# Retention: state updates of four batches as 32-row products on four row tiles

## The chip, the cores and the metric

The kernel runs on one core of a Trainium2 chip. The metric is the device time of one execution in microseconds (us), as the median of several runs. The engines appear as PE (TensorE), DVE (VectorE), ACT (ScalarE), POOL (GpSimd) and SP (SyncE, which here only issues DMAs).

## The reference

One inference step of a decoder trunk of two layers, for one prompt of 256 tokens and eight samples of 4 tokens each (256 + 32 = 288 token columns). Layer 0 mixes by causal pooling, layer 1 by retention; each layer then has a convolutional FFN and a gated embedding. What the change touches is the retention of the samples, for each of 8 heads with key width 256 and value width 512:

```python
sc = jnp.einsum('bhnk,bhmk->bhnm', qc, kc) * intra
o = (jnp.einsum('bhnm,bhmv->bhnv', sc, vc)
     + jnp.einsum('bhnk,bhkv->bhnv', qc, S) * cross[None, :, :, None])
S = sdec[None, :, None, None] * S + jnp.einsum('bhmk,bhmv->bhkv', kc * kdec[None, :, :, None], vc)
```

For the samples, `S` is a given state of 256 x 512 for each of the 8 batches and 8 heads, and the new one is an output: 64 states of 512 KB are read, used and written. `o` is then normalised over its 512 values, multiplied by `silu(g)` and projected.

## The kernel before

All matrix work keeps weights stationary and moves the 288 token columns. Every float32 operand is split into a high and a low part of type fp32r, and `three` (line 270) issues three products: high x high, high weight x low, low weight x high. A weight piece of 256 x 512 is loaded (`dma`, line 1429, on SP, five buffers), split by ScalarE (`split_hi`, line 1435) and VectorE (`split_lo`, line 1443), two pieces ahead of its use. The main loop goes through the pieces in order; for each of 4 output blocks `m` it issues six products and then calls `tick`. A `Group` is a set of pieces with the same output; it holds four PSUM banks, from a pool of five (`pbank`), and is emptied by `evac` at its last piece.

Everything else is side work: short operations in two queues, `main` and `side`, which `tick` drains into the instruction streams between main products. The planner keeps an estimated clock per engine. An operation is written down if its PSUM need `nb` is met and it is `timely`: a TensorE operation when its inputs are due by TensorE's clock, another one when its inputs and its engine's clock are at most 500 ns ahead. One drain stops after 900 ns of TensorE work:

```python
while q and q[0].eng != "W" and fits(q) and timely(q[0]) and pe < 900:
    if q[0].eng == "P":
        pe += q[0].cost
    run(q)
```

The order thus written is what each engine executes; real waits are semaphores. Side work draws banks from a second pool of three (`sbank`, first in, first out); `release` puts a bank back at the moment when the last reader is written down, and the hardware waits for that reader.

In retention, a head has a group for q and k (`gA`), one for v (`gB`), four short ones of 4 row blocks for the output projection of head h-2 (`gO`), and one for the gate (`gC`). `attention` (from line 1041) queues the side work of a head. The sample keys and values are stacked four times into 128 rows (a high or low part of all 32 tokens in each 32 rows: `kst`, `vsk`), transposed on TensorE and kept as `ksr` and `vst`. Then, for each batch `b` and each half `kk` of the key width: `sh_` and `sl_` split the state half, `upd` (line 1258) multiplies `Km`, which is `ksr` masked to the rows of batch b (`km_`, line 1254), with `vst`, all 128 rows; `outer` (lines 1274, 1275) adds q x state into one bank `os`, held through all 16 halves; `snew` (line 1262) forms the new state from the old one and the update bank and frees the bank; a store goes out on POOL (line 1265) and the load of a later state on SP (line 1051), three state buffers in all. At the end `osum0` and `osum1` (lines 1324, 1327) bring the output to the tile `on[2]` of 32 rows, `gstat` and `gnorm` normalise, and `otrans` transposes four column blocks, each with two transposes of 128 rows and one of 32 (through line 268). `norm_ops` (lines 321, 322) spreads the row norms with a product of ones; its last part has 32 rows.

Of the kernel before, what the change touches and what calls it, by code (L numbers as in the profile page):

```python
# [32 lines left out]
RAW_BUFS = 5  # L33
SPLIT_BUFS = 3
# [11 lines left out]
def _constants():  # L46
# [39 lines left out]
    c["dm"] = np.where(n >= m, np.exp(lg[:, None, None] * np.maximum(n - m, 0)) / 16, 0).astype(f)  # L86
# [4 lines left out]
    c["gx"] = np.exp(lg[:, None] * (t + 1)[None, :]).astype(f)  # L91
    c["ks"] = (np.exp(lg[:, None] * (3 - t)[None, :]) / 16).astype(f)
# [3 lines left out]
    c["ds"] = np.tile(ds, (4, 1, 1)).astype(f)  # L96
    c["bm"] = np.tile((b[:, None] == np.arange(8)[None, :]).astype(f), (4, 1))
# [14 lines left out]
def trunk_kernel(ctx: ExitStack, tc: tile.TileContext, I: dict, O: dict):  # L112
# [5 lines left out]
    mmp = ctx.enter_context(tc.tile_pool(name="mmp", bufs=5, space=bass.MemoryType.PSUM))  # L118
    msp = ctx.enter_context(tc.tile_pool(name="msp", bufs=1, space=bass.MemoryType.PSUM))

    def pbank():
        return mmp.tile([128, 512], F32, tag="mm", name="mm")

    banks = [msp.tile([128, 512], F32, name=f"ms{i}") for i in range(3)]
    free = deque(banks)

# [23 lines left out]
    side = deque()  # L150
    ready = set()
# [3 lines left out]
    class Op:  # L155
        __slots__ = ("eng", "cost", "fn", "nb", "key", "dep", "end")

        def __init__(self, eng, cost, fn, nb=0, key=None, dep=()):
            self.eng, self.cost, self.fn, self.nb, self.key, self.dep, self.end = eng, cost, fn, nb, key, dep, 0.0

# [34 lines left out]
    def fits(q):  # L195
        op = q[0]
        return op.nb <= len(free) and (op.key is None or op.key in ready)

    def inputs(op):
        return max((d.end for d in op.dep), default=0.0) + LAT  # L200
# [27 lines left out]
    def tick():  # L228
        drain(main)
        drain(side)  # L230

    def step():
        if main and fits(main):
            run(main)
        elif side and fits(side):
            run(side)
        else:
            raise RuntimeError("nothing can run")

    def force(cond):  # L240
        while not cond():
            step()

# [54 lines left out]
    def norm_ops(ph, dep=()):  # L298
# [68 lines left out]
    class PoolPhase:  # L367
# [47 lines left out]
        def start(self):  # L415
# [11 lines left out]
            px = pbank()  # L427
# [15 lines left out]
            for _ in range(16):  # L443
# [10 lines left out]
                   px.rearrange("p (j c t) -> p c j t", j=4, c=4))  # L454
            w = self.weigh(1) + self.sbg(1)
# [17 lines left out]
        def xT(self, i, q, on_v):  # L473
            ps = pbank()
# [103 lines left out]
    class FfnPhase:  # L578
# [3 lines left out]
        def start(self):  # L582
            force(lambda: not side and "rows" in ready)
# [188 lines left out]
    class PlePhase:  # L772
# [3 lines left out]
        def start(self):  # L776
            force(lambda: not side and ("u", self.l, 21) in ready)
# [31 lines left out]
        def build(self):  # L809
# [26 lines left out]
            def finish():  # L836

                flush()
                sums = [pbank() for _ in range(3)]
# [14 lines left out]
                for m in range(4):  # L854
                    ps = sbank() if m < 3 else pbank()
# [79 lines left out]
    class RetPhase:  # L935
# [5 lines left out]
        def start(self):  # L941
            force(lambda: not side and "x15" in ready)
# [7 lines left out]
            self.gx, self.ks = t("gx", [128, HEADS, 32]), t("ks", [128, HEADS, 32])  # L950
            self.ds, self.bm = t("ds", [128, HEADS, 32]), t("bm", [128, 8])
            GP.dma_start(self.kd, I["kd"])
            GP.dma_start(self.gx, I["gx"].partition_broadcast(128))
            GP.dma_start(self.ks, I["ks"].partition_broadcast(128))
            GP.dma_start(self.ds, I["ds"])
# [3 lines left out]
            GP.memset(self.qb.bitcast(F32), 0.0)  # L959
            self.mv = t("mv", [128, 3, 2])  # L960
# [7 lines left out]
            self.kst = t("kst", [128, 2, 4, 32])  # L968
            self.krp = t("krp", [128, 2, 4, 32])
# [4 lines left out]
            self.vsk = t("vsk", [128, 4, 4, 32])  # L974
            self.vst = t("vst", [128, DV], F32R)
            self.ssf = t("ssf", [128, 32])
            self.ssh = t("ssh", [128, 32], F32R)
            self.sss = t("sss", [128, 32], F32R)
            self.bn = t("bn", [128, 3, 6])
# [63 lines left out]
        def attention(self, h):  # L1043
# [5 lines left out]
            def load_s(b):  # L1049
                s = self.tl("S", [128, 2, DV], 3)  # L1050
                SP.dma_start(s, I["state_ret"][0, b, h].rearrange("(k p) v -> p k v", p=128))
                st["S", b] = s
                ld = Op("D", 0, None)
                at = max(clk["P"], stored[b - 3].end + 2500 if b >= 3 else 0.0)
                ld.end = charge("D", PIECE, at) + 2000
                loaded[b].dep = loaded[b].dep + (ld,)


            def loads():
                st["dm"] = self.tl("dm", [128, 256], 1)  # L1060
                SP.dma_start(st["dm"], I["dm"][h])
                load_s(0)
                load_s(1)
            bc = lambda t: t[:, h].unsqueeze(1).broadcast_to([128, 2, 32])
# [6 lines left out]
            kr = lambda: st["kr"].bitcast(F32)  # L1071
# [8 lines left out]
            loaded, stored = {}, {}  # L1080
            ops.append(Op("N", 0, loads))
            add("krp", oa(256, lambda: A.copy(self.krp, ks.unsqueeze(2).broadcast_to([128, 2, 4, 32]))), "rot")
# [429 lines left out]
```

## Time and profile before

| | |
|---|---|
| median of 3 runs | 3006.28 us (3005.09 to 3008.97) |
| profiled execution | 3006.09 us, span 3004.2 us |
| PE busy | 2985.6 us (99%) |
| PE weight loads busy | 2934.2 us (98%) |
| DVE busy | 1957.9 us (65%) |
| ACT busy | 1415.4 us (47%) |
| POOL busy | 80.7 us (3%) |
| DMA | 542.08 MB, mean 180 GB/s |

The span runs from the first to the last instruction of the profiled execution; its own time also holds what lies around it. Busy shares are means over the whole span. A product's row on PE shows its whole passage through the array; products are pipelined, so the next one starts long before the row ends, and the distance between starts tells what a product costs.

### The profile page before, as it was taken

To read this page: it belongs to the slowest core of one execution; us is meant where nothing else is said; L and a number is where in the kernel's file an instruction comes from. 1 tells how busy PE (TensorE), PEld (TensorE's weight loads), DVE (VectorE), ACT (ScalarE), POOL (GpSimd) and SP (SyncE) were. 2 spreads that over 40 slices of the span, in tenths; PEclk is the share of its full clock that TensorE was granted. 3 is DMA by queue.
4 is the path that set the end of the run, shared out by engine and by line. 5 is a ranking of instruction groups with operands and counts; after the bars stand their busy time and mean duration, and the time that the engine had idled before them with its cause. 6 is when DMAs were issued, how large, how long until landed. Compare 5 with 4: busy or idle time off the path is not lost.

```text
span 3004.2 us, 54263 instructions
## 1 busy us (share of the span) xinstructions
PE 2985.6 (99%) x22007; PEld 2934.2 (98%) x22007; DVE 1957.9 (65%) x3401; ACT 1415.4 (47%) x2142; POOL 80.7 (3%) x129
## 2 busy tenths in 40 slices
PE   8999999999999999999999999999999999999998
PEld 8999999999999999999999999999999999999998
DVE  7666656565666666776766767686666575756565
ACT  6544444444444545444444444455444343434454
POOL 1000000000000000000000000000000000000000
PEclk9999999999999999999999999999999999999999
DMA  7555555555555566665756757565555555555553
GB/s 231 158 164 166 168 162 167 163 166 164 167 175 165 168 217 198 233 232 164 249 192 207 231 170 247 191 192 172 163 167 168 164 165 166 165 166 165 175 159 116
DMA packets 288817, 542.08 MB, mean 180 GB/s; under 512 B 18836, under 2 KB 55652, under 8 KB 288454
## 3 DMA queue, kind: packets, MB, share of 16 engines
q1 hardware_dynamic: 275878, 496.21, 53.6%
q0 software_dynamic: 12688, 42.40, 4.2%
q8 instruction: 173, 2.83, 0.4%
q14 instruction: 78, 0.64, 0.1%
HBM read 496.41 MB, written 42.84 MB: 179 GB/s over the span
## 4 chain that ended last, share of the span: by engine, by line
PE 98%; DMA 1%; DVE 0%; ACT 0%; issue 0%; SPq 0%; ACTq 0%; DVEq 0%
PE mm L271 31%; PE mm L273 30%; PE mm L272 30%; PE ms L268 1%; PE ms L1274 1%; PE ms L1258 1%; PE ms L1275 1%; PE ms L272 0%; PE ms L271 0%; PE ms L273 0%; DMA raw<-in_ret_w_in 0%; PE ms L1090 0%; DMA x<-in_x_prompt 0%; DVE lo L1443 0%; PE mm L268 0%
## 5 line engine op out<-in xcount | busy, mean ns | idle before, releaser
L1435 ACT CAST hi<-raw 128x1024 fp32r<-128x1024 f32 x864 | 907.5, 1050 | 1391.0 <-PE mm L272 1190.8
L271 PE MATMUL mm<-xh,hi 128*128 128x288 f32 x4928 | 1464.4, 297 | 0.0
L272 PE MATMUL mm<-xl,hi 128*128 128x288 f32 x4928 | 1453.9, 295 | 0.0
L273 PE MATMUL mm<-xh,lo 128*128 128x288 f32 x4928 | 1449.1, 294 | 0.0
L1443 DVE TENSOR_TENSOR lo<-raw,hi 128x1024 fp32r<-128x1024 f32 x864 | 1055.7, 1222 | 552.2 <-ACT hi L1435 550.2
L271 PEld LDWEIGHTS mm<-xh,hi 128*128 128x128 f32 x4928 | 923.8, 187 | 11.8
L272 PEld LDWEIGHTS mm<-xl,hi 128*128 128x128 f32 x4928 | 925.3, 188 | 4.7
L273 PEld LDWEIGHTS mm<-xh,lo 128*128 128x128 f32 x4928 | 927.9, 188 | 0.0
L272 PE MATMUL mm<-hl,hi 128*128 128x288 f32 x1408 | 415.4, 295 | 0.0
L273 PE MATMUL mm<-hh,lo 128*128 128x288 f32 x1408 | 415.1, 295 | 0.0
L271 PE MATMUL mm<-hh,hi 128*128 128x288 f32 x1408 | 413.3, 294 | 0.0
L271 PEld LDWEIGHTS mm<-hh,hi 128*128 128x128 f32 x1408 | 264.7, 188 | 0.0
L272 PEld LDWEIGHTS mm<-hl,hi 128*128 128x128 f32 x1408 | 264.7, 188 | 0.0
L273 PEld LDWEIGHTS mm<-hh,lo 128*128 128x128 f32 x1408 | 264.5, 188 | 0.0
L665 DVE SCALAR_TENSOR_TENSOR c<-U,cv,c 128x304 f32<-128x304 f32 x352 | 180.2, 532 | 3.5 <-ACT c L662 0.4
L271 PE MATMUL mm<-rhh,hi 128*128 128x288 f32 x512 | 152.2, 297 | 0.0
L273 PE MATMUL mm<-rhh,lo 128*128 128x288 f32 x512 | 151.5, 296 | 0.0
L272 PE MATMUL mm<-rhl,hi 128*128 128x288 f32 x512 | 149.8, 293 | 0.4 <-DVE rhl L1352 0.4
L755 DVE TENSOR_TENSOR x<-x,mm 128x288 f32<-128x288 f32 x192 | 82.7, 452 | 86.2 <-PE mm L273 86.2
L637 DVE TENSOR_TENSOR U<-mm,rb 128x256 f32<-128x256 f32 x176 | 74.2, 422 | 94.7 <-PE mm L273 94.7
L662 ACT ACTIVATE c<-U,cv 128x304 f32<-128x304 f32 x176 | 107.7, 635 | 15.7 <-DVE U L638 15.7
L1262 DVE SCALAR_TENSOR_TENSOR S<-S,ms 128x512 f32<-128x512 f32 x128 | 87.4, 683 | 36.1 <-PE ms L1258 35.8
(265 smaller groups left out, 2110.8 us busy)
## 6 DMA issues: line engine op xcount, KB each, us to landing
raw<-in_ffn_w_up SPq DMA_DIRECT2D x352, 512.0 KB
raw<-in_ffn_w_down SPq DMA_DIRECT2D x176, 512.0 KB
raw<-in_ret_w_in SPq DMA_DIRECT2D x128, 512.0 KB
raw<-in_ple_w_gate SPq DMA_DIRECT2D x64, 512.0 KB
raw<-in_ret_w_in SPq DMA_DIRECT2D x128, 256.0 KB
S<-in_state_ret SPq DMA_DIRECT2D x64, 512.0 KB
out_ret_s<-S POOLq DMA_DIRECT2D x64, 512.0 KB, 4.4
raw<-in_ret_w_out SPq DMA_DIRECT2D x64, 512.0 KB
```

The lines of the kernel that those rows point to most:

```text
L268: T.transpose(out, in_, ident[:rows, :rows])
L271: T.matmul(out, w[0], a[0], start=start, stop=False)
L272: T.matmul(out, w[0], a[1], start=False, stop=False)
L273: T.matmul(out, w[1], a[0], start=False, stop=stop)
L637: V.tensor_tensor(U[:, s, 2:258], ps[:, 0:256], rb[:, 0:256], MUL)
L662: A.activation(c[0][:, 0:304], u[:, 2:306], AF.Identity, bias=w(3), scale=w(2))
L665: V.scalar_tensor_tensor(c[0][:, 0:304], u[:, s:304 + s], w(s), c[0][:, 0:304], MUL, ADD)
L755: V.tensor_tensor(x[:, M], x[:, M], ps[:, :NT], ADD)
L1258: T.matmul(ps, st["km", b][:, 128 * kk:128 * kk + 128], self.vst, start=True, stop=True)
L1262: V.scalar_tensor_tensor(s[:, kk], s[:, kk], g ** 4, st["u", b, kk], MUL, ADD)
L1435: A.copy(h, raw[i])
L1443: V.tensor_tensor(l, r, h.bitcast(F32), SUB)
```

## The change

- The two PSUM pools become one of eight banks. Main groups take theirs from it too; `kept` reserves those that the current group has yet to take.
- The stacks are ordered by row tile: the 32 rows of tile r hold the high and low parts of batches 2r and 2r+1. `Km` is `ksr` masked to the even or the odd batch of each tile, two masks in place of eight. `upd(par, kk)` issues four products of 32 rows, one for each tile, each into a bank of its own.
- The state halves are tiles of their own, eight buffers, loaded through a third queue, `back`; they go in the order of the update groups. The output is summed in four groups of four halves, each in a bank that `osum` adds to a resident tile `on2` of 128 rows; `fold` adds its rows 32 to 63 to rows 0 to 31. State updates of a group follow among the outputs of the next.
- `otrans` transposes all 128 rows of `on2`; the last part of the spread in `norm_ops` has 128 rows.
- The tables `dm`, `gx`, `ks`, `ds` of a head come in one load `hd`; `kst`, `krp` and `vsk` share a tile; in the last head the fourth update group goes behind the transposes; phases start with `finish_side` in place of a forced drain.

```diff
+    banks = [psp.tile([128, 512], F32, name=f"ps{i}") for i in range(8)]
     free = deque(banks)
+    kept = [0]
...
-        return op.nb <= len(free) and (op.key is None or op.key in ready)
+        return op.nb <= len(free) - kept[0] and (op.key is None or op.key in ready)
...
         drain(main)
         drain(side)
+        drain(back)
...
-            V.tensor_scalar(diag[:32, 256:288], ident[:32, :32], rtok[:32, 2:3], None, MUL)
+            V.tensor_scalar(diag[:, 256:288], ident[:, 0:32], rtok[:, 2:3], None, MUL)
...
-            T.matmul(ps[:, 256:288], ones[:32, :], diag[:32, 256:288], start=True, stop=True)
+            T.matmul(ps[:, 256:288], ones, diag[:, 256:288], start=True, stop=True)
...
+            self.hd = self.tl("hd", [128, 352], 1)
+            SP.dma_start(self.hd, I["hd"][h])
...
+            def load_s(n, dep=()):
+
+                b, kk = where(n)
+                ld = Op("D", PIECE / 2, None, dep=dep, late=3500.0 if dep else 0.0)
...
+            def upd(par, kk):
+                for r in range(4):
+                    rows = slice(32 * r, 32 * r + 32)
+                    ps = st["u", 2 * r + par, kk] = sbank()
+                    T.matmul(ps, st["km", par][rows, 128 * kk:128 * kk + 128], self.vst[rows], start=True, stop=True)
+
+            def snew(n):
+                b, kk = where(n)
+                V.scalar_tensor_tensor(st["S", n], st["S", n], g ** 4, st["u", b, kk], MUL, ADD)
                 release(st["u", b, kk])
...
+                GP.dma_start(O["ret_s"][0, b, h, 128 * kk:128 * kk + 128], st["S", n])
+
+                if n + S_BUFS < 16:
+                    load_s(n + S_BUFS, (o[f"sn{n}"],))
...
+            def outer(n):
+                b, kk = where(n)
+                if n % 4 == 0:
                     st["os"] = sbank()
                 o = st["os"]
                 lq = self.qb[:, kk, 64 * b:64 * b + 64]
...
+                T.matmul(o[:64], lq, st["sh", n], start=n % 4 == 0, stop=False)
+                T.matmul(o[:64], lq, st["sl", n], start=False, stop=n % 4 == 3)
...
+            def osum(u):
+                if u == 0:
+                    A.copy(self.on2[:64], st["os"][:64])
+                else:
+                    V.tensor_tensor(self.on2[:64], self.on2[:64], st["os"][:64], ADD)
+                release(st["os"])
...
+            def new_state(n):
+                add(f"sn{n}", ov(512, lambda: snew(n)), f"up{n // 4}")
+
+            def update(u):
+                add(f"up{u}", op_(430, lambda: upd(u // 2, u % 2), nb=4), "km1 vsk")
+
+            for u in range(4):
+                for n in range(4 * u, 4 * u + 4):
+                    if u > 0:
+                        new_state(n - 4)
+                    add(f"out{n}", op_(460 + (230 if n == 0 else 0), lambda n=n: outer(n), nb=0 if n % 4 else 1),
+                        f"sl{n}" + (" sss vsk" if n == 0 else ""))
+                    if n < 14:
+                        half(n + 2)
+                        half_lo(n + 2)
+                add(f"os{u}", (oa if u == 0 else ov)(512, lambda u=u: osum(u)), f"out{4 * u + 3}")
+                if u < 3 or h < 7:
+                    update(u)
+            add("fold", ov(512, fold), "os3")
...
-                to_tr(ps[:, 256:288], on[2][:32, c], 32)
+                to_tr(ps[:, 256:384], on[2][:, c], 128)
...
             for m in range(4):
                 if j == 0:
-                    g.ps[m] = pbank()
+                    g.ps[m] = sbank()
+                    kept[0] -= 1
...
                     g.evac(m, ps)
+                    release(ps)
```

## Rows read from the trace of the kernel before

**Rows 1.** The page, parts 1 and 4: busy time, chain that ended last.
```profile
PE 2985.6 (99%) x22007; PEld 2934.2 (98%) x22007; DVE 1957.9 (65%) x3401; ACT 1415.4 (47%) x2142; POOL 80.7 (3%) x129
...
PE 98%; DMA 1%; DVE 0%; ACT 0%; issue 0%; SPq 0%; ACTq 0%; DVEq 0%
```

**Rows 2.** One head's stretch: length, PE, PEld, DVE, ACT, POOL busy; clock; DMA.
```profile
1510.00:1634.00 124.00, 124.00 (x880) 118.23 (x879) 85.17 (x148) 58.46 (x89) 6.40 (x9) 1.00 0.65 209
```

**Rows 3.** Waits of PE: who waited for whom, total us, times, longest.
```profile
PE mm L268 <- DMA ident<-in_ident: 5.3, 1, 5.3
...
PE ms L504 <- DVE xl L521: 0.7, 1, 0.7
...
PE mm L272 <- DVE rhl L1352: 0.4, 1, 0.4
```

**Rows 4.** PE by line and form: count, busy us, mean ns, idle before.
```profile
L1258 PE MATMUL ms<-vst,Km 128*128 128x512 f32 x128 | 50.4, 394 | 0.0
...
L268 PE MATMUL ms<-ident,fm 128*128 128x128 f32 x64 | 8.3, 272 | 0.0
...
L268 PE MATMUL ms<-ident,on 32*128 32x32 f32 x32 | 7.8, 244 | 0.0
...
L321 PE MATMUL ms<-acc,ones 128*128 128x256 f32 x10 | 3.1, 388 | 0.5 <-DVE acc L316 0.5
```

**Rows 5.** Timeline of PE in the state work of head 0: start, length, instruction.
```profile
1137.09 0.40 PE L1258 MATMUL ms<-vst,Km 128*128 128x512 f32 x1
...
1138.48 0.29 PE L271 MATMUL mm<-xh,hi 128*128 128x288 f32 x1
1138.61 0.29 PE L272 MATMUL mm<-xl,hi 128*128 128x288 f32 x1
```

**Rows 6.** Timeline of PE at one `otrans`; x3 are merged: two 128-row, one 32-row.
```profile
1151.27 0.55 PE L268 MATMUL ms<-ident,on 128*128 128x128 f32 x3
...
1151.76 0.40 PE L271 MATMUL mm<-xh,hi 128*128 128x288 f32 x1
...
1151.99 0.29 PE L272 MATMUL mm<-xl,hi 128*128 128x288 f32 x1
```

**Rows 7.** Timeline of PE: eight transposes of 128 rows, merged.
```profile
1079.49 1.03 PE L268 MATMUL ms<-ident,fm 128*128 128x128 f32 x8
```

**Rows 8.** Timeline of PE at one spread in `norm_ops`; two 32-row products between.
```profile
79.97 0.59 PE L321 MATMUL ms<-acc,ones 128*128 128x256 f32 x2
...
81.06 0.30 PE L272 MATMUL mm<-xl,hi 128*128 128x288 f32 x1
```

**Rows 9.** Timeline, all engines: an update product and its state update.
```profile
1096.16 0.39 PE L1258 MATMUL ms<-vst,Km 128*128 128x512 f32 x1
...
1096.59 0.69 DVE L1262 SCALAR_TENSOR_TENSOR S<-S,ms 128x512 f32<-128x512 f32 x1
```

**Rows 10.** The same with a weight split of DVE between them.
```profile
1104.62 0.40 PE L1258 MATMUL ms<-vst,Km 128*128 128x512 f32 x1
...
1105.90 0.68 DVE L1262 SCALAR_TENSOR_TENSOR S<-S,ms 128x512 f32<-128x512 f32 x1
```

**Rows 11.** Line L1262 (`snew`): what DVE sat idle for before it, us, times.
```profile
  PE ms L1258: 35.8, 33
```

**Rows 12.** Timeline in the pooling layer: PE waits for a bank that DVE empties.
```profile
23.46 0.18 DVE L521 TENSOR_TENSOR xl<-ms,xh 128x32 fp32r<-128x32 f32 x1
...
23.70 0.30 PEld L504 LDWEIGHTS ms<-pq,x 128*128 128x128 f32 x2 [0.86 <-DVE xl L521]
```

**Rows 13.** DVE by line and form: count, busy us, mean ns, idle before.
```profile
L1254 DVE TENSOR_SCALAR Km<-ksr,bm 128x256 fp32r<-128x256 f32 x64 | 22.9, 358 | 0.0
...
L1015 DVE TENSOR_TENSOR qk<-fm,t 128x576 f32<-128x576 f32 x8 | 6.0, 752 | 0.0
...
L1327 DVE TENSOR_TENSOR on<-on,ms 32x512 f32<-32x512 f32 x8 | 5.4, 669 | 0.0
```

**Rows 14.** Waits of SP's DMA queue: state loads behind state stores.
```profile
SPq L1051 <- DMA out_ret_s<-S: 149.1, 40, 7.4
```

More of the change, by code (lines that the diff above doesn't have):

```diff
@@ L117, in trunk_kernel @@
     wp = ctx.enter_context(tc.tile_pool(name="wp", bufs=1))
[L118 to L124, printed above, removed]
+    psp = ctx.enter_context(tc.tile_pool(name="psp", bufs=1, space=bass.MemoryType.PSUM))
+    banks = [psp.tile([128, 512], F32, name=f"ps{i}") for i in range(8)]
     free = deque(banks)
+    kept = [0]
     def sbank():
@@ L150, in trunk_kernel @@
     side = deque()
+    back = deque()
     ready = set()
@@ L196, in fits @@
         op = q[0]
-        return op.nb <= len(free) and (op.key is None or op.key in ready)
+        return op.nb <= len(free) - kept[0] and (op.key is None or op.key in ready)
     def inputs(op):
-        return max((d.end for d in op.dep), default=0.0) + LAT
+        return max((d.end for d in op.dep), default=0.0) + LAT + op.late
     def run(q):
@@ L236, in step @@
             run(side)
+        elif back:
+            run(back)
         else:
@@ L242, in force, with finish_side @@
             step()
+    def finish_side():
+        while side:
+            if side[0].eng == "W":
+                side.popleft()
+            elif fits(side):
+                run(side)
+            else:
+                step()
     def force_key(k):
@@ L582, in start @@
         def start(self):
-            force(lambda: not side and "rows" in ready)
+            finish_side()
+            force_key("rows")
             l = self.l
@@ L776, in start @@
         def start(self):
-            force(lambda: not side and ("u", self.l, 21) in ready)
+            finish_side()
+            force_key(("u", self.l, 21))
             l = self.l
@@ L838, in finish @@
                 flush()
-                sums = [pbank() for _ in range(3)]
+                sums = [sbank() for _ in range(3)]
                 toks = (slice(0, 128), slice(128, 256), slice(256, 288))
@@ L941, in start @@
         def start(self):
-            force(lambda: not side and "x15" in ready)
+            finish_side()
+            force_key("x15")
             p = self.p = new_pool("ret")
@@ L977, in start @@
             self.ssh = t("ssh", [128, 32], F32R)
+            self.ssg = t("ssg", [128, 32])
             self.sss = t("sss", [128, 32], F32R)
+            self.on2 = t("on2", [128, DV])
+            V.memset(self.on2, 0.0)
             self.bn = t("bn", [128, 3, 6])
@@ L1047, in attention, with where, load @@
             st = {}
[L1049 to L1056, printed above, removed]
-            def loads():
[L1060 to L1064, printed above, removed]
+            dm, gx, sk, ds = (self.hd[:, a:b] for a, b in ((0, 256), (256, 288), (288, 320), (320, 352)))
+            bc = lambda t: t.unsqueeze(1).broadcast_to([128, 2, 32])
+            def where(n):
+                return 2 * (n % 4) + n // 8, (n // 4) % 2
+            def load_s(n, dep=()):
+                b, kk = where(n)
+                ld = Op("D", PIECE / 2, None, dep=dep, late=3500.0 if dep else 0.0)
+                def load():
+                    st["S", n] = self.tl("S", [128, DV], S_BUFS)
+                    SP.dma_start(st["S", n], I["state_ret"][0, b, h, 128 * kk:128 * kk + 128])
+                    here = Op("D", 0, None)
+                    here.end = ld.end + 2000
+                    o[f"sh{n}"].dep += (here,)
+                    ready.add(("S", h, n))
+                ld.fn = load
+                back.append(ld)
+            def loads():
+                for n in range(S_BUFS):
+                    load_s(n, self.stored[n:n + 1])
             qv = [self.qb[:, kk].rearrange("p (b c) -> p b c", c=68) for kk in range(2)]
@@ L1368, in attention @@
             ops += hid
+            if h == 7:
+                update(3)
+                for n in range(12, 16):
+                    new_state(n)
             side.extend(ops)
```

175 lines of the change are left out of this document (82 added, 93 removed).

## Prediction

> **What bounds the kernel now.** The page comes first: TensorE is busy 99% of the span and the chain that ended last is 98% TensorE [rows 1]. Then the table by stretches: in the retention layer one head takes 124 us, TensorE is busy in all of it, VectorE 85 us of it, at the full granted clock [rows 2]. Then TensorE's own waits: the longest are 5.3 us at the start and 0.7 us in the pooling layer, and the only one in retention is 0.4 us [rows 3]. So TensorE is never late: every nanosecond taken from its stream shortens the run, and every nanosecond for which it must wait lengthens it. Work on VectorE, ScalarE and the queues is free until TensorE waits for it. I therefore sum TensorE's stream and new waits. The sum is made against the profiled execution, 3006.09 us (span 3004.2 us plus 1.9 us around it), which stands 0.2 us below the median of the three runs, 3006.28.
>
> **Updates as row tiles.** There are 128 update products [rows 4]. In the timeline two updates and four output products run from 1137.09 to 1138.48, 1.39 / 6 = 0.232 us a product [rows 5]: 128 x 0.232 = 29.7 us, or 0.93 us for the four that become one group. After, there are 32 groups of four products of 32 rows.
>
> A change between 128 and 32 rows costs time. The transposes of one output column block are three, the last one of 32 rows. From the first of them to the second main product after them it takes 1151.99 - 1151.27 = 0.72 us [rows 6]. Eight 128-row transposes in a row take 1.03 us, less 0.27 for the last one's own length: 0.11 each [rows 4, 7]; a main product takes 0.13 [rows 5]. In one mode the same would take 3 x 0.11 + 0.13 = 0.46, so one excursion into 32 rows costs 0.26 us beyond a product's place, 0.37 with it. A 512-column product streams 480 columns more than that 32-column one; from 0.13 for 288 columns to 0.232 for 512 is 0.45 ns a column, so 0.21 us. A group whose four tiles overlap fully takes 0.37 + 0.21 = 0.58 us; 32 x 0.58 = 18.6, that is **-11.1 us**. Bounds, since no row shows several row tiles at once: with no cost for the mode, 32 x 0.23 = 7.4 us (-22.3); with tiles strictly one after the other, 32 x (0.58 + 3 x 0.232) = 40.8 us (+11.1). I take 0.58, nearest to the one excursion that a row shows.
>
> The Trainium skill, TensorE: Matmul & The Clock Gate, Part 3 (measured speedup), gives 3.07x for four row tiles of 32 rows and 512 columns. By it a group would take 0.30 us and the term would be an estimated -20 us instead of -11.1; no row here shows such a group.
>
> **128-row transposes.** The 32 transposes of `on2` [rows 4] lose the excursion: 32 x 0.26 = **-8.3 us**. The 96 columns more cost nothing, because 0.11 is already the pace of 128-column ones. The broadcast in `norm_ops` loses one too: from 79.97 to 81.06 stand two 256-column products (0.20 apart: 0.59 for both less 0.39 for one), two 32-row ones and a main product, 1.09 us; in one mode 2 x 0.20 + 2 x 0.11 + 0.13 = 0.75 [rows 4, 8]. Five norms x 0.34 = **-1.7 us**.
>
> **The new wait.** The pool has eight banks, the main group holds four, so `up` (nb=4) takes all that are left. It can run only after `osum` has given back the output bank. The next output group `out4`, `out8`, `out12` needs a bank, and the only one is that which `snew` of the first state of this update frees. `release` is bookkeeping: the bank counts as free when VectorE's instruction is written down, but TensorE really waits for it. `drain` then writes `up`, `sn`, `out` behind each other: `out` depends on `sl` only, long ready, and 430 is below its limit of 900. Queued behind the waiting product are all main products, since TensorE runs in order. In the kernel before two banks take turns and `up` never needs the bank just read.
>
> The price: of the 0.26 us of an excursion, 0.11 are weights that nothing hides after a mode change (the main product behind it lasts 0.40 in place of 0.29 [rows 6]). The same 0.11 stand ahead of the first tile, and of the rest I put 0.09 on the entry, so it streams 0.20 us into the group. From a product's start to its state update it is 0.43 us when VectorE is free (1096.16 to 1096.59) [rows 9], 1.28 when a weight split stands between (1104.62 to 1105.90) [rows 10]. The state update lasts 0.69 [rows 9], and in 33 of 128 cases VectorE stood waiting for the product [rows 11]. VectorE's end to the next weight load is 23.70 - (23.46 + 0.18) = 0.06 us [rows 12], and the weights are exposed, 0.11. Together 0.20 + 0.43 + 0.69 + 0.06 + 0.11 = 1.49 us, 0.91 beyond the 0.58 of the group.
>
> There are three such turns a head, 24. Not each costs this. If the planner's VectorE clock is over 500 ahead, `sn` goes to the next tick and six main products (0.8 us) come between; and in the last piece of a main group an evacuated main bank is spare (half the ticks of the four-row-block groups of `gO`). I take 14 turns in full and 10 at 0.1: 12.7 + 1.0 = 13.7 us. The fourth group of a head waits only with its last tile, for `osum` of the group just ended; 7 of these (head 7 has none there) at 0.2: 1.4 us. **+15.1 us** in all. Bounds: nothing, if main work always comes between; 24 x (0.91 + 0.4) + 7 x 0.9 = 37.7 us if each turn waits and VectorE comes 0.4 late, half of the 0.85 between [rows 9] and [rows 10].
>
> **What lies beside.** VectorE loses 48 of 64 `Km` instructions of 0.36 us (-17 us) and gains 16 more `osum` and 8 `fold` of 0.67 (+16) [rows 13], so it stays at about 85 of 124 us; ScalarE has one copy more a head. State loads become 128 halves on SP, written down 3.5 us after the planned store. SP now waits 149 us for stores [rows 14] without TensorE noticing, because raw pieces are five deep; that cover also holds 64 more issues. If it were gone, TensorE would wait in `L1429`'s pieces. POOL issues 128 stores instead of 64, on an engine that is busy 6.4 of 124 us [rows 2]. `hd` replaces `dm` and three resident tables: it is issued at `qk_done`, and six rotation instructions of 0.75 us on VectorE [rows 13] hide its landing; uncovered, VectorE stops, and the two split pieces ahead are the next cover. `ssg`, the strided `kst` and the shared `stk` tile stay on engines with room. All at nothing. In `PoolPhase.start` eight banks in place of three may remove the 0.7 us wait of L504 for a bank [rows 3]: **-0.7** (0 to -0.7). The last head's 0.4 us at the hand-over to `gO(7)` may go, as four state updates now follow the transposes: **-0.4**, within 2 us either way, because this side work is just in time.
>
> **Sum:** -11.1 - 8.3 - 1.7 + 15.1 - 0.7 - 0.4 = -7.1; 3006.1 - 7.1 = **2999 us**.
>
> **Rivals.** A: no turn waits, because something always stands between `up` and `out`. For it: in the kernel before the planner keeps TensorE from every such wait. Against it: nothing in `out`'s dependencies names `sn`. Then -22.2: 2984 us.
>
> B, slower: the return of the bank decides everywhere. Mechanism: all 24 turns wait, and VectorE, with `osum` right ahead of `sn`, comes 0.4 us late, with all 7 last tiles at 0.9: +37.7 - 22.2 = +15.5, 3022 us. From 22.2 us of waits (0.66 us for each of 24 turns and 7 last tiles at 0.9) the change is a loss. For it: 1.28 us in [rows 10]; against it: the 0.43 in [rows 9], and VectorE has a third of its time free. The Trainium skill, TensorEngine Tiling (Array Packing), Performance Considerations (PSUM bottleneck), warns of just this: tiling speeds TensorE but not the emptying of PSUM, which may become the bound; no run here shows it yet.
>
> C: the tiles don't overlap. A turn that waits hides it (0.58 + 0.70 = 1.28, below 1.49), the other 18 groups pay 0.70: 2999 + 12.6 = 3012 us. For it: no row shows overlap; against it: neither does one exclude it.
>
> **Chances.** Forecast 0.40, A 0.20, B 0.23, C 0.17. A measurement of this kernel tells 0.2%, 6 us, from no change: faster is below 3000.3, slower above 3012.3. The forecast's own range is 2991 to 3007: faster 0.26, same 0.14. A gives faster 0.20. B, from 3008 up, gives slower 0.17, same 0.06. C gives same 0.11, slower 0.06. Sum: faster 0.46, same 0.31, slower 0.23. The range, 2984 to 3018, takes in the forecast and C and reaches to A's value and into B.
>
> **What would show it.** Right: TensorE rows of `out` waiting for VectorE's `S`, some 14 times by about 0.9 us, TensorE idle in the retention stretches for the first time; groups of four update rows that start within some 10 ns of each other, with 0.58 us from the last main product's end to the next where nothing waits; no 32-row transpose of `on2`, and 0.46 where [rows 6] have 0.72. Wrong: update rows 0.2 us apart (C), no waits (A), over 25 waits (B), or a wait for `hd` or a state load, which I have at nothing.

## The result and the profile after

The change made the kernel slower: 3024.7 us (median of 6 runs, 3021.3 to 3026.3) against 3007.1 us (median of 6 runs beside them), a ratio of 1.0053 with a 95% interval of 1.0039 to 1.0067. The profiled execution took 3022.2 us, 16.1 us more than the one that the prediction was worked out from.

The page of the changed kernel, part 1, answers to [rows 1]. TensorE has 7.8 us less work in it than before, in a span that is 16.2 us longer: 24 us went into time in which it does nothing.

```profile
PE 2977.8 (99%) x22007; PEld 2927.1 (97%) x22007; DVE 1962.1 (65%) x3386; ACT 1414.1 (47%) x2142; POOL 103.1 (3%) x190
```

The stretch of [rows 2] in the changed kernel (length, busy time of PE, PEld, DVE, ACT, POOL, granted clock, DMA share, GB/s): TensorE, busy in all 124 us before, now stands idle for 2.8 us of them. VectorE has about the load that the prediction gave it.

```profile
1510.00:1634.00 124.00, 121.18 (x873) 115.55 (x872) 87.32 (x151) 60.69 (x94) 11.00 (x20) 1.00 0.67 217
```

TensorE's waits in the changed kernel (who waited for whom, us in total, times, longest) answer to [rows 3]. Two lines are new in retention's turns, L1328 (`out`, for the state update `snew`) and L1309 (the update, for the sum `osum`); L1398 is the norm ahead of head 7's transposes.

```profile
PE ps L1328 <- DVE S L1313: 11.3, 14, 0.9
PE ps L1309 <- DVE on L1337: 7.3, 10, 1.2
...
PE ps L288 <- ACT on L1398: 4.6, 3, 4.1
PE ps L341 <- DVE acc L337: 1.5, 1, 1.5
...
PE ps L293 <- DVE lo L1511: 0.7, 1, 0.7
```

**A group with no wait.** Timeline of TensorE (start, length, instruction; rows of one form are merged, x4): the four products of 32 rows pass within 0.50 us, and one alone is as long (the x1 rows of two turns below), so the tiles run side by side. From the main product ahead to the second one behind it is 1687.16 - 1686.27 = 0.89 us, less 2 x 0.13 for two main products: 0.63. Four products cost 0.93 before.

```profile
1686.27 0.30 PE L293 MATMUL ps<-xh,lo 128*128 128x288 f32 x1
...
1686.50 0.50 PE L1309 MATMUL ps<-vst,Km 32*128 32x512 f32 x4
1686.93 0.40 PE L291 MATMUL ps<-xh,hi 128*128 128x288 f32 x1
...
1687.16 0.29 PE L292 MATMUL ps<-xl,hi 128*128 128x288 f32 x1
```

**A turn that waits for the state update.** Timeline of TensorE and VectorE. VectorE is free (it has waited 2.78 us) and starts 0.52 us after the tiles; 0.69 us later the bank is back, and `out` starts 0.06 us after that. From the end of the main product's own 0.13 us (1568.09) to `out` it is 1.37 us. With what the pair then loses at its own start, such a turn costs 1.42 to 1.49.

```profile
1567.96 0.29 PE L293 MATMUL ps<-xh,lo 128*128 128x288 f32 x1
1568.19 0.51 PE L1309 MATMUL ps<-vst,Km 32*128 32x512 f32 x4
1568.71 0.69 DVE L1313 SCALAR_TENSOR_TENSOR S<-S,ps 128x512 f32<-128x512 f32 x1 [2.78 <-PE ps L1309]
...
1569.46 0.45 PE L1328 MATMUL ps<-Sh,qb 128*64 128x512 f32 x1 [0.76 <-DVE S L1313]
```

Before, VectorE sat waiting for the update product in 33 of 128 cases [rows 11]. Now the view of line L1313 shows fewer, but they are the first ones of a turn, with TensorE behind them:

```profile
  PE ps L1309: 22.3, 16
```

**A turn whose last tile waits for the sum.** The same two engines. Three tiles run; the fourth needs the bank that `osum` (L1337) gives back. On VectorE a weight split of 1.22 us stands ahead of `osum`, so the fourth tile comes 1.61 us behind the first. There are five such turns, 2.24 to 2.32 us each.

```profile
1466.58 1.22 DVE L1511 TENSOR_TENSOR lo<-raw,hi 128x1024 fp32r<-128x1024 f32 x1
1466.62 0.29 PE L293 MATMUL ps<-xh,lo 128*128 128x288 f32 x1
...
1466.84 0.50 PE L1309 MATMUL ps<-vst,Km 32*128 32x512 f32 x3
1467.72 0.67 DVE L1337 TENSOR_TENSOR on<-on,ps 64x512 f32<-64x512 f32 x1
...
1468.45 0.50 PE L1309 MATMUL ps<-vst,Km 32*128 32x512 f32 x1 [1.11 <-DVE on L1337]
```

**A fourth group.** Here `osum` can't start before the last output product is through, even with VectorE free. The last tile comes 0.84 us late; five of the seven groups look like this one.

```profile
1609.26 0.50 PE L1309 MATMUL ps<-vst,Km 32*128 32x512 f32 x3
1609.36 0.68 DVE L1337 TENSOR_TENSOR on<-on,ps 64x512 f32<-64x512 f32 x1 [0.89 <-PE ps L1329]
...
1610.10 0.50 PE L1309 MATMUL ps<-vst,Km 32*128 32x512 f32 x1 [0.34 <-DVE on L1337]
```

**The transposes.** Where [rows 6] have 0.72 us, it is now 1630.29 - 1629.83 = 0.46:

```profile
1629.83 0.49 PE L288 MATMUL ps<-ident,on 128*128 128x128 f32 x3
...
1630.29 0.29 PE L292 MATMUL ps<-xl,hi 128*128 128x288 f32 x1
```

**Head 7.** TensorE, ScalarE and VectorE ahead of the last output group `gO(7)`. The main products end at 1999.04, the norm's numbers are there at 2002.42, and the first transpose runs at 2003.32: 4.1 us with nothing to do. Before, these transposes ran from 1986 to 1993 with main work between them. From the first output product to the last, head 7 now takes 63.3 us in place of 49.7; the other heads 47 to 58 in place of 43 to 46.

```profile
1998.91 0.29 PE L293 MATMUL ps<-rhh,lo 128*128 128x288 f32 x1
...
2002.26 0.16 DVE L1394 SCALAR_TENSOR_TENSOR nb<-mv,rs 128x3 f32<-128x3 f32 x1
2002.45 2.22 ACT L1398 ACTIVATE on<-on,nb,rs 128x512 f32<-128x512 f32 x3 [2.30 <-DVE nb L1394]
2003.32 0.47 PE L288 MATMUL ps<-ident,on 128*128 128x128 f32 x1 [4.12 <-ACT on L1398]
```

**The clock.** The table by stretches, in columns as above, of the three places inside the run where the granted clock is half (before, there was none but at the very end). Each stands behind a wait: the turns at 1115 and 1971 us, 2.3 us each, and the wait for the norm. A main product costs 0.24 us there in place of 0.13, so half of the busy time is lost: (3.4 + 3.4 + 4.4) / 2 = 5.6 us.

```profile
1117.40:1120.80 3.40, 3.40 (x14) 3.08 (x14) 2.25 (x3) 0.00 (x0) 1.08 (x2) 0.51 0.59 182
1974.10:1977.50 3.40, 3.40 (x17) 3.40 (x16) 1.92 (x3) 0.00 (x0) 0.00 (x0) 0.50 0.43 145
2001.40:2008.20 6.80, 4.42 (x18) 3.83 (x19) 3.62 (x13) 3.88 (x7) 0.00 (x0) 0.50 0.11 42
```

**The hand-over to the next layer.** Head 7's four state updates come at its very end, 2034 us; their stores leave at 2035 to 2037. VectorE's first instruction of the next layer, L624, writes into space that the state buffers held, and waits 3.48 us for a store. A weight split is queued behind it, and TensorE's main product behind that. Before, no such row stands on VectorE.

```profile
2034.40 1.88 DVE L1313 SCALAR_TENSOR_TENSOR S<-S,ps 128x512 f32<-128x512 f32 x3
...
2036.18 1.07 POOL L1315 DMA_DIRECT2D out_ret_s<-S  x2 [0.27 <-issue]
...
2039.77 0.07 DVE L624 MEMSET U<- 128x16 f32 x1 [3.48 <-DMA out_ret_s<-S]
2039.83 1.23 DVE L1511 TENSOR_TENSOR lo<-raw,hi 128x1024 fp32r<-128x1024 f32 x1
...
2041.11 0.40 PE L293 MATMUL ps<-xh,lo 128*128 128x288 f32 x1 [0.73 <-DVE lo L1511]
```

SP's waits for state stores, 149.1 us in 40 before [rows 14], grew, but no wait of TensorE goes back to the load of a weight piece:

```profile
SPq L1087 <- DMA out_ret_s<-S: 202.7, 55, 6.8
```

### The profile page after: what moved, and what is told of

Its sections match the earlier page's. It is cut to its first block, busy times and chain, and to the rows that moved or that the text cites. A ratio compares the mean times of both kernels' runs of the same rounds, so it can differ in the third digit from the quotient of the medians.

```text
span 3020.4 us, 54435 instructions
## 1 busy us (share of the span) xinstructions
PE 2977.8 (99%) x22007; PEld 2927.1 (97%) x22007; DVE 1962.1 (65%) x3386; ACT 1414.1 (47%) x2142; POOL 103.1 (3%) x190
## 5 line engine op out<-in xcount | busy, mean ns | idle before, releaser
L291 PE MATMUL ps<-xh,hi 128*128 128x288 f32 x4928 | 1465.6, 297 | 0.1
L292 PE MATMUL ps<-xl,hi 128*128 128x288 f32 x4928 | 1454.7, 295 | 0.0
L293 PE MATMUL ps<-xh,lo 128*128 128x288 f32 x4928 | 1450.0, 294 | 0.8 <-DVE lo L1511 0.7
L291 PEld LDWEIGHTS ps<-xh,hi 128*128 128x128 f32 x4928 | 924.1, 188 | 15.2 <-issue 3.6
L292 PEld LDWEIGHTS ps<-xl,hi 128*128 128x128 f32 x4928 | 925.9, 188 | 5.4
L293 PEld LDWEIGHTS ps<-xh,lo 128*128 128x128 f32 x4928 | 928.7, 188 | 1.3 <-DVE lo L1511 1.2
L292 PE MATMUL ps<-hl,hi 128*128 128x288 f32 x1408 | 415.4, 295 | 0.0
L293 PE MATMUL ps<-hh,lo 128*128 128x288 f32 x1408 | 415.1, 295 | 0.0
L291 PE MATMUL ps<-hh,hi 128*128 128x288 f32 x1408 | 413.3, 294 | 0.0
L291 PEld LDWEIGHTS ps<-hh,hi 128*128 128x128 f32 x1408 | 264.7, 188 | 0.0
```

The lines of the kernel that those rows point to most:

```text
L291: T.matmul(out, w[0], a[0], start=start, stop=False)
L292: T.matmul(out, w[0], a[1], start=False, stop=False)
L293: T.matmul(out, w[1], a[0], start=False, stop=stop)
```

## The experiments

Each kernel ran beside the kernel before on one chip; the ratio is to that. The last three columns are from each kernel's profiled execution: how much later (+) or earlier (-) than in the kernel before TensorE starts the first main product of `gO(6)` (1963.5 us before), the first of the next layer (2019.4) and the last of all (2988.1). They tell in which of three stretches the time went. Side work that a kernel moves past one of these points shows as a shift between two columns.

| kernel | median us (runs) | ratio, 95% interval | gO(6) | next layer | last |
|---|---|---|---|---|---|
| changed kernel | 3024.7 (6) | 1.0053, 1.0039 to 1.0067 | +4.0 | +14.2 | +16.7 |
| e1_due | 3021.5 (5) | 1.0043, 1.0031 to 1.0056 | -33.3 | +10.3 | +13.5 |
| e2_tr128 | 2999.0 (7) | 0.9971, 0.9960 to 0.9982 | -5.9 | -6.6 | -7.2 |
| e3_full | 3019.9 (4) | 1.0037, 1.0024 to 1.0051 | +1.1 | +9.6 | +12.0 |
| e4_late0 | 3042.4 (4) | 1.0109, 1.0094 to 1.0125 | +40.8 | +38.5 | +40.8 |
| e5_out | 3012.4 (11) | 1.0015, 1.0007 to 1.0024 | -7.5 | +2.2 | +6.6 |
| e6_out3250 | 3009.9 (11) | 1.0006, 0.9998 to 1.0015 | -7.7 | -4.7 | +4.9 |
| e7_early | 3015.5 (7) | 1.0027, 1.0015 to 1.0038 | -2.8 | +0.2 | +8.1 |
| e8_late2500 | 3028.7 (4) | 1.0066, 1.0052 to 1.0079 | +10.8 | +12.4 | +21.4 |
| e9_up3 | 3004.4 (11) | 0.9986, 0.9977 to 0.9995 | -12.7 | -9.7 | -0.3 |
| e10_last | 3004.3 (11) | 0.9984, 0.9975 to 0.9993 | -13.8 | -4.4 | -1.5 |
| e11_force | 2996.1 (5) | 0.9955, 0.9943 to 0.9968 | -11.4 | -8.4 | -9.0 |
| e12_force2 | 2999.4 (8) | 0.9972, 0.9961 to 0.9982 | -11.6 | -5.8 | -6.5 |

**e1_due: both waits of the turns taken away, by the order alone.** The changed kernel with two dependencies more: `up` is written down only after `osum`, the first `out` of a group only after the `sn` that frees its bank.

```
-  add(f"up{u}", op_(430, lambda: upd(u // 2, u % 2), nb=4), "km1 vsk")
+  add(f"up{u}", op_(430, lambda: upd(u // 2, u % 2), nb=4), f"km1 vsk os{u}")
...
-              f"sl{n}" + (" sss vsk" if n == 0 else ""))
+              f"sl{n}" + (" sss vsk" if n == 0 else "") + (f" sn{n - 4}" if u > 0 and n % 4 == 0 else ""))
```

> The planner is told of the two banks: `up` also depends on `os` of the same group, `out4`, `out8`, `out12` also on the state update that frees their bank. Nothing else changes, so each engine has the same instructions in another order. Theory 1 (the waits for banks are the loss): the 25 turns that cost 24.7 us above the 0.64 of a group without a wait go to nearly nothing, and the half-clock stretches behind them go too: 2990 to 2998 us, waits of TensorE for `S` and `on` under 3 us. Theory 2 (the loss is the last head's late side work and the half clock there; the bank waits are paid back elsewhere): the state work comes later still, the wait before `gO(7)` grows beyond 4 us: 3012 us or more.

The time is Theory 2's. In heads 0 to 6 every group costs 0.63 or 0.64 us: the waits are gone. But a head's output products now spread over 62 to 73 us, and the side work falls behind from head to head. Head 7's first output product starts at 1952 us, in place of 1925 in the changed kernel, and its work has to be forced out ahead of `gO(7)`, with no main product left between. TensorE's waits, and the stretch of half clock, by the table by stretches:

```profile
PE ps L1328 <- ACT Sh L1347: 11.7, 8, 3.4
PE ps L288 <- ACT on L1398: 6.6, 3, 6.1
```

```profile
1970.90:2005.00 34.10, 17.14 (x43) 8.21 (x44) 20.19 (x45) 8.89 (x15) 4.86 (x9) 0.50 0.43 147
```

So there are two losses with one root: a turn has a chain of its own, sum, update, state update, next output product. Either TensorE stands in it, or the order waits for it and the last head has no cover.

**e2_tr128: the transposes and the norm's spread alone.** The kernel before, with `on2` as a zeroed tile of 128 rows and products of 128 rows.

```
-  T.matmul(ps[:, 256:288], ones[:32, :], diag[:32, 256:288], start=True, stop=True)
+  T.matmul(ps[:, 256:288], ones, diag[:, 256:288], start=True, stop=True)
...
-  to_tr(ps[:, 256:288], on[2][:32, c], 32)
+  to_tr(ps[:, 256:384], on[2][:, c], 128)
```

> The kernel before with one part of the change alone: transposes of `on2` and the last part of the spread in `norm_ops` with 128 rows. Step 3 of the prediction right: the 32 transposes go from 0.72 to 0.46 us each with the product behind, -8.3, and the spread -1.7: 2996 to 2999 us against 3006 to 3007. Rival (the excursion is cheap or hidden): within 2 us of the kernel before.

0.9971 of 3008 us is 8.7 us less, with an interval of 5.4 to 12.0; its profiled execution has 7.1 us less span. The prediction's 10.0 us for these two edits lie inside the interval. With this part alone the kernel is faster than before and after the change.

**e3_full: the same turns without row tiles.** The update products of the changed kernel on 128 rows, which sums the four batches into each state, so the state output is another; every size but the rows stays.

```
-  T.matmul(ps, st["km", par][rows, 128 * kk:128 * kk + 128], self.vst[rows], start=True, stop=True)
+  T.matmul(ps, st["km", par][:, 128 * kk:128 * kk + 128], self.vst, start=True, stop=True)
```

> The changed kernel with update products of all 128 rows in place of 32: each sums the four batches of its parity, so the new states are wrong; the same instructions and the same order otherwise. Theory 1 (the turn is set by the state update on VectorE, so what the row tiles save is lost in the wait): a group without a wait costs 0.93 instead of 0.64 us, but a turn that waits has its first product 0.2 us earlier: within 6 us of the changed kernel, 3019 to 3027 us. Rival (the change between row modes is the loss): 3010 us or less. Second rival (the row tiles' saving reaches the end): +9, 3033 us.

The time is inside Theory 1's range. Groups without a wait cost 0.92 to 0.93 us in place of 0.64, as four products of 128 rows did before. Groups that wait for the state update cost 1.22 to 1.29 in place of 1.42 to 1.49, those that wait for the sum behind a split 2.04 to 2.13 in place of 2.24 to 2.32. All 32 together take 42.3 us against 45.1 with row tiles. In the changed kernel's order the row tiles thus saved nothing: what they make shorter is the part of the chain that the wait covers, and the entry into 32 rows is added to it.

**e4_late0: state loads written down with no delay.** `late=3500.0` becomes `late=0.0`; the turns stay.

> The changed kernel with state loads written down 3.5 us earlier (late 0.0). Theory 1: the turns wait as before, within 4 us of the changed kernel, 3020 to 3028 us. Theory 3 (state loads that are put off make the state work longer, 48 to 63 us a head in place of 43 to 50, and that makes the last head late): the last head's state work shortens by some 8 us, the 4.1 us wait before `gO(7)` and the half clock behind it go: 3014 to 3017 us.

Neither theory: the wait for the norm ahead of `gO(7)` went, but this kernel is the slowest of all. TensorE's waits:

```profile
PE ps L1309 <- DVE on L1337: 28.7, 12, 4.2
...
PE ps L1328 <- DVE S L1313: 4.8, 12, 0.9
```

The load now stands on SP's queue while its store is still under way (longest wait of SP for a store 13.6 us, in place of 6.8). What comes late is the state half: ScalarE waits 113.2 us in 46 cases for state loads, in place of 10.6 us in 11.

```profile
ACT Sh L1347 <- DMA S<-in_state_ret: 113.2, 46, 5.1
```

The timeline of one turn follows the chain to its end. VectorE's split of the low part waits behind ScalarE's of the high part, a weight split and `osum` (L1337) stand behind it on VectorE, and the fourth tile, 4.4 us behind the first, waits for `osum`:

```profile
1344.70 0.62 ACT L1347 CAST Sh<-S 128x512 fp32r<-128x512 f32 x1 [3.79 <-DMA S<-in_state_ret]
...
1345.35 0.69 DVE L1353 TENSOR_TENSOR Sl<-S,Sh 128x512 fp32r<-128x512 f32 x1 [4.07 <-ACT Sh L1347]
...
1347.10 0.67 DVE L1337 TENSOR_TENSOR on<-on,ps 64x512 f32<-64x512 f32 x1
...
1347.82 0.49 PE L1309 MATMUL ps<-vst,Km 32*128 32x512 f32 x1 [3.90 <-DVE on L1337]
```

So some delay, costed at nothing in the prediction, was needed. At 3.25 us ScalarE's waits for state loads are 6.6 us (e6), at 2.5 us they are 64.4 us (e8).

**e5_out: only the first `out` of a group waits in the order.** The second of e1's two lines.

> Changed kernel, with one dependency more: the first output product of a group (out4, out8, out12) is written down only after the state update (sn0, sn4, sn8) that frees its bank. Theory 1 (the bank's return is the loss): the 14 waits of TensorE for VectorE's S, 11.3 us in the changed kernel, go; the 7.3 us of waits of a last tile for the sum L1337 and the 4.1 us ahead of gO(7) stay; 3011 to 3015 us. Theory 2 (what is taken from a wait in the early heads comes back as late side work in head 7, as with both dependencies at once): 3019 us or more, with more time at half clock near the end.

The time is inside Theory 1's range. The 11.3 us of waits for the state update are gone altogether, and the median is 12.3 us lower than that of the changed kernel. All 32 groups take 32.9 us, 12.2 less than 45.1. The other two waits stayed:

```profile
PE ps L1309 <- DVE on L1337: 6.4, 10, 1.1
PE ps L288 <- ACT on L1398: 5.5, 3, 5.0
```

Most of the loss that e1 moved into head 7 came from its other line, then: head 7 starts at 1914 us here.

**e6_out3250: and a little less delay for the loads** (`late=3250.0`).

> As the run before, and the state loads are written down 3.25 in place of 3.5 us (planned time) after the store that frees their buffer, so that the planner has no side work of head 7 left over ahead of gO(7). Theory 1 with the tail as a second, separate loss: the 4.1 us wait ahead of gO(7) and the half clock around it go as well, some 8 us less than the run before: 3002 to 3008 us. Rival: the shorter lead lets SP stand behind stores that have not landed, as when the delay was 0; then waits for L1337 grow and it is 3015 us or more.

The wait for the norm went, and the first main product of the next layer starts 6.9 us earlier than in e5. But only 1.7 us of that were left at the end, and 3009.9 us lies above the expected range: from there on this kernel loses 9.6 us against the kernel before. So the tail is a loss of its own, and behind it stands another, the hand-over, that a late tail had hidden. The rival's sign did not come: the waits for L1337 fell to 3.9 us in 7 cases.

**e7_early: the sum and the update ahead of the halves.** With e5's line, `os` and `up` stand right behind the fourth output product of a group.

> As the run with the one dependency, and the sum L1337 and the next update stand right behind the fourth output product, ahead of the halves of the next state. Theory 1: no wait for S, but every last tile of the 31 groups that follow an output group waits for the sum itself, 0.5 to 0.8 us each, 15 to 25 us; no side work is left over ahead of gO(7): 3012 to 3024 us. Rival (main products come between the sum and the update by themselves): waits under 5 us, 3000 to 3005 us.

Theory 1, in its time as well: the waits for the state update are gone, last tiles wait for the sum in 20 listed cases, and all groups take 37.6 us, 4.7 more than in e5. Moving the sum earlier moves the update with it, and the distance between them, which is what the last tile needs, stays as short.

**e8_late2500: the changed kernel with a delay of 2.5 us.**

> Changed kernel with state loads written down 2.5 in place of 3.5 us after the store; turns untouched. Theory (the tail is a loss of its own, worth about 8 us with its half clock): waits for S and L1337 stay at 18 to 19 us, the wait ahead of gO(7) goes, 3014 to 3019 us. Rival (SP then stands behind stores, loads come late): waits at the updates grow by more than is won, 3024 us or more.

The wait for the norm went here too, but the turns of the third update grew to as much as 4.4 us, and waits of 6.2 us in the next layer came in. That is the rival's way, at a smaller delay than that of e6. It also shows that the delay is one part of the length of a head: in heads 0 and 1 the output products take 45 us in place of 50.5 and 56.5. Heads 3 and 4 take 55 and 51 in place of 49 and 47.5, so a shorter delay does not shorten every head.

**e9_up3: the fourth update behind its sum.** As e6, and in heads 0 to 6 `up3` depends on `os3`. No output product of that head comes behind it.

> As the run with 3.25 us, and in heads 0 to 6 the fourth update (up3) is written down only after the sum os3 that it needs. Theory: the fourth groups with the sum written down behind them (1.46 us in five of seven heads) fall to 0.63, 4.2 us less, and nothing comes back because no output product follows in that head: 3004 to 3007 us. Rival: the updates come later, the next head's state loads with them, and head 7 is again left over ahead of gO(7): 3009 us or more, with ScalarE's L1398 among TensorE's waits.

All fourth groups cost 0.64, and nothing came back: the time is inside the expected range. At `gO(6)` this kernel is 12.7 us ahead of the kernel before and at the start of the next layer 9.7, but in the end only 0.3. TensorE's waits at that hand-over, 2010 to 2060 us, and VectorE's:

```profile
PE ps L341 <- DVE acc L336: 3.2, 1, 3.2
PE ps L293 <- DVE lo L1511: 1.7, 1, 1.7
PE ps L292 <- DVE xl L314: 1.6, 1, 1.6
```

```profile
DVE U L624 <- DMA out_ret_s<-S: 3.9, 1, 3.9
```

With 6.8 us at half clock behind the last of them (2.9 us for 5.83 us busy) these are 9.4 us, the whole loss.

**e10_last: the last state updates earlier.** As e9, and head 7's fourth update follows its output products, its four `sn` follow the norm instead of the transposes.

> As the run before, and the fourth update of head 7 is issued right after its output products, its four state updates behind the norm, in place of behind the transposes. Theory (the hand-over to the next layer is a loss of its own: VectorE's L624 waits 3.5 to 3.9 us for the last state stores, because the buffers change hands, and TensorE then waits for halves and for acc, with half clock): VectorE's wait at L624 goes, TensorE's waits between 2000 and 2070 us (6.5 us in the run with 3.25 us) fall under 3, and no half clock there: 4 to 8 us less than the run before, 2997 to 3003 us. Rival: VectorE's four updates, 2.7 us, come ahead of the transposes that the last output group gO(7) needs, and TensorE waits there instead: no gain, within 2 us of the run before.

The rival came. VectorE's wait at L624 is gone, but its 2.7 us of updates now stand ahead of what `gO(7)` needs, and TensorE waits there:

```profile
PE ps L291 <- ACT rhh L1428: 4.1, 2, 2.7
```

Two stretches of half clock follow it (6.8 us from 1982 and 3.4 us from 1992). Between `gO(6)` and the next layer this kernel loses 9.4 us, as e9 does one stretch later. A third stretch of half clock, 3.4 us at 2043.6, is left in the next layer, where the expectation had none.

**e11_force and e12_force2: the last state updates between both.** As e9; the four `sn` are written down at the latest ahead of the second (e11) or third (e12) column block of `gO(7)`.

```
-  lambda k: force_key(("rh", h, k)), evac))
+  lambda k, mq=mq: force_key(("rh", h, k) if h < 7 or k or mq != 1 else ("last",)), evac))
```

> The kernel of the run with up3 behind os3 (3004.35), with one more point: the four state updates of head 7 are written down at the latest ahead of the second column block of gO(7), some 15 us after the transposes, in place of at the end of the layer. Theory (hand-over to the next layer is a loss of its own; in the run before, the first main product of the next layer starts 9.8 us earlier than before the change, the last one only 0.4): the wait of VectorE's L624 for stores goes, TensorE's waits in 2000 to 2070 (6.5 us) and the half clock there too, and nothing stands ahead of the transposes: 2994 to 2999 us. Rival: the updates hold up VectorE's other work in gO(7), TensorE waits for its banks or halves and the clock falls there: 3002 us or more.

> The same, at the latest ahead of the third column block of gO(7). Same theory: 2994 to 2999 us, if the stores still land ahead of the end of the layer; else between that and 3004.

e11 is the fastest kernel of this study, 0.45% below the kernel before, and its ratio is 0.16% below that of e2, though the two intervals overlap. TensorE has no wait at all from 1990 to 2080 us and no half clock there; what it waits for between 1974 and 2010 is:

```profile
PE ps L291 <- ACT rhh L1431: 2.0, 2, 1.0
```

e12, at 2999.4, misses the first of its two ranges by 0.4 us and falls into the second; it has a wait of 2.3 us in `gO(7)` that e11 hasn't:

```profile
PE ps L293 <- DVE lo L1513: 2.3, 1, 2.3
```

## Why the prediction was wrong

By its own steps, in us of the profiled execution:

| step | predicted | measured | from |
|---|---|---|---|
| groups without waits | -11.1 | -9.1 | 32 x 0.64 against 29.6 |
| transposes and spread | -10.0 | -8.7 | e2 |
| 14 turns that wait for the state update | +12.7 | +11.4 | 1.42 to 1.49 each |
| the other 10 turns | +1.0 | +8.9 | five for the sum (8.1), two for a bank that ScalarE empties (0.8), three none |
| fourth groups | +1.4 | +4.3 | 7 groups |
| start | -0.7 | -1.6 | first main product; e5, with the same start, has +0.6 |
| head 7 ahead of `gO(7)` | -0.4 | +4.6 | wait for L1398 |
| clock | 0 | +5.6 | three stretches |
| hand-over to the next layer | 0 | +2.5 | last two columns of the table |

The measured steps sum to 17.9, against 16.1 for the two executions: 1.8 us are not placed, and the interval of e2 alone is wider than that.

**What held.** The tiles overlap, so rival C is out. A group costs 0.64 in place of 0.58. The Trainium skill, TensorE: Matmul & The Clock Gate, Part 3, has 3.07x for four row tiles of 32 rows and 512 columns. Here, between other products, it is 0.93 / 0.64 = 1.45x, and the trace decides. The three-transpose block came out at the very 0.46 that was worked out. The mechanism of the new wait was right and so was its price: 1.42 to 1.49 us against 1.49, and e5 took exactly this away by naming `sn` in `out`'s dependencies. The number of such turns, 14 forecast and 14 measured, is in part luck: no row stood behind it.

**The step that failed: "The new wait", at its second half.** It saw that a bank counts as free when VectorE's instruction is written down, and that TensorE really waits for it, but it drew the list of waits from `out` alone. The same holds for the bank that `osum` gives back and the fourth tile takes. The prediction had this only in the fourth groups, at 0.2 us, and put the turns that don't wait for the state update at 0.1. It let a turn go free when VectorE is behind; in five of those the weight split that put VectorE behind stood ahead of the sum, at 1.6 us. Of the 24 turns 14 wait for the state update, five for the sum, two, 0.3 and 0.5 us long, for a bank that ScalarE empties, and three for nothing: half of what escapes the one wait falls into the other. In all the waits came to 24.6 us in place of 15.1, beyond the 22.2 us from which the prediction let the change become a loss. That is rival B's side, but by another way than B had: VectorE was not late at the state updates, it was late at the sums. That B's 3022 us is also the measured time is luck: B has 37.7 us of waits, 13.1 more than measured, and nothing for head 7, the clock and the hand-over.

**The other step that failed: "What lies beside ... All at nothing", and "within 2 us either way" for head 7.** The prediction looked at engines' loads, and these came out as it said. It did not follow the order that the planner makes of the longer chain. Head 7's output products took 13.6 us longer, there was no main work left to cover its norm, and the last state stores ran into the next layer. From `gO(6)` to the end the kernel lost 16.7 - 4.0 = 12.7 us, waits and the half clock behind them taken together; 3.4 us of these belong to the turn at 1971 us and the half clock behind it. e5, e9 and e11 take the three losses away one after the other: the waits for the state update, those of the fourth groups, the hand-over; e6 takes the tail. By the last main product the loss goes from 16.7 us to 6.6 (e5), 4.9 (e6), -0.3 (e9) and -9.0 (e11).

**What of rival B's warning.** The Trainium skill, TensorEngine Tiling (Array Packing), Performance Considerations, says that the emptying of PSUM may become the bound when tiles speed up TensorE. The trace agrees with that for a turn (bank returned 1.2 us after the tiles start, tiles 0.51 us long), and e3 shows the consequence: with the waits in place, products on all rows took 42.3 us in the turns and row tiles 45.1. It is no property of the tiles alone: in e11, with the same tiles and a better order, all 32 groups take 27.4 us, 2.2 less than the 29.6 of the old updates. That is what was reached of the 11.1 us that the prediction gave the tiles. In time e11 and e2, which has the old updates, are not told apart: their intervals overlap.

**Left open.** Why a head's output products spread further was not taken apart: the delay of the loads is part of it (e8), the wait for four free banks may be another. In e11 the groups of the second and third updates still cost 7.0 us more than 0.64 each; this was not removed, since the dependency that removes it in all turns costs more at head 7 (e1).

## What to carry to other kernels

When a change lets one instruction take all the banks that are left, list every instruction that gives one of them back and what stands ahead of each on its engine; a product that is started too early stops all products behind it. Naming the true releaser in the order was worth as much here as the faster product (12.3 us against 9.1), but only where work is left to fill the gap: look at the last head, where it isn't. A load that is written down before its space is free holds up what stands behind its readers (e4). Follow the last stores of a layer into the next one's buffers.

## What the runs showed of the hardware that was not expected

The granted clock fell to half (1.2 in place of 2.4 GHz) behind some waits of TensorE, for 3.4 or 6.8 us, and in e1, where TensorE had side work alone, for 34.1 us. Among these waits are turns of 2.3 us in which TensorE stood idle for only 1.1 to 1.2 us (1115 and 1971 us). It did not fall behind others of nearly the same length: the turns at 1467, 1720 and 1846 us cost 2.24 to 2.25 us each and have no such stretch behind them. In e6 the turns at 1116 and 1463 us cost 2.24 us each, and the clock fell behind the first alone; what decides is not shown. In a kernel that keeps TensorE busy at 99%, a wait of 4.1 us therefore cost some 6: 4.1 and half of the 4.42 us busy at half clock. Four products of 32 rows and 512 columns on four row tiles started so close together that the merged row is 0.50 or 0.51 us long, against 0.50 for one.
